# Row sums of a feed-forward input taken two places earlier, and one corner product of a Strassen pair split in halves around the second sum's product

## The chip, the core and the metric

The kernel runs on one core of one Trainium2 chip. The core has a matrix engine (TensorE, PE in the profile), a vector engine (DVE), a scalar engine (ACT), GpSimd (POOL) and a queue engine (SP), each with its own queue of instructions, and 16 DMA engines. The metric is the device time of one execution in microseconds. Three runs of the kernel before took 1920.91 to 1923.19 us, with a median of 1921.95 us. A change of about 0.2% is what such runs can tell from none.

## The reference, cut to what matters

Two layers, each a feed-forward network, a token mixing, and a second feed-forward network. The change touches the feed-forward input alone:

```
def swiglu(x, w_in, w_out):
    gate, up = jnp.split(x @ w_in, 2, axis=-1)
    return (jax.nn.silu(gate) * up) @ w_out
...
hn = rms_norm(h, g_ffn1[l]) * (1.0 + sc1) + sh1
h = h + 0.5 * (1.0 + gt1) * swiglu(hn, w_ffn1_in[l], w_ffn1_out[l])
```

There are 512 tokens, a model width of 1024 and a hidden width of 2816, that is 22 tiles of 128 hidden rows. All is float32.

## The kernel before

**Products.** A float32 operand is split into a high part (a rounded cast, on ACT, `nc.scalar.copy`) and a low part (the rest, a subtraction on DVE); `split`, lines 100 to 102, does both. A product then takes three passes through the matrix engine: high by high, high weights by low input, low weights by high input. Each weight tile of 128x1024 needs one cast on ACT and, after it, one subtraction on DVE before its third pass can run; the split pairs `wH` and `wL` live in a ring of four.

**A feed-forward input** (`ffn`, line 364). The hidden tiles come in pairs `p`, two tiles `j` to a pair. The first `n_first` pairs are multiplied directly: for each `j` a gate tile `pg` and an up tile `pu` come from the generator `projector` (line 278), then a block (lines 513 to 517) makes silu(gate) times up and splits it into `actH` and `actL`. `n_first` is 4 in the first feed-forward network, whose weights begin to arrive at the start of the program, and 2 in the other three. Their first three direct tiles are multiplied during the step before, so five follow in the network itself, each of 48 passes of 256 columns.

**The Strassen pairs.** All later pairs go through `pair_in` (line 449), which computes gate and up tiles of a pair with seven half-size products in place of eight. `prod` (line 436) is one such product: 2 hidden tiles by 4 row tiles by 3 passes, 24 passes of 256 columns. On the input side the products need sums and differences of rows of the input, `P1`, `P2`, `T3` and `T4`, made once for each network on DVE: `whole(0)` and `whole(1)` (line 406) join high and low parts of the rows again, four instructions each; `combine` (line 414) makes one of the four with two instructions and then splits it (one cast on ACT, one subtraction on DVE). On the weight side a pair loads four quarter tiles `A(i, k)`, two of them with an accumulating DMA on POOL (`plus`), and forms sums on DVE (lines 464 and 474).

One pair in order, before the change: `S`=A10+A11 by P1 into `pF` (line 457); copy `up` from `pF`; A00 (`a11`) by rows B11 into `pD` (461); copy `s1` from `pD` on ACT (463); `S` plus a11 on DVE (464); `flush()`, which runs the last product of the pair before (T4, line 486); `S` by P2 on top of `pD` (466); copy `s2` from `pD` (468); A01 (`a12`) by B21 into `pG` (470), the corner product; `gate` from `pG` and `s1` (472); `S` plus a12 (474); `S3` by T3 on top of `pD` (477); `S` by B22 into `pF` (479). `S` by P2 may not write `pD` before `s1` has been copied out of it. In the first Strassen pair nothing waits to be flushed.

**When the sums are made.** `when` (line 502) gives each of the six pieces a place `m` among the direct tiles: `beside(2 * j)` comes between `pg` and `pu` of tile `j`, `beside(2 * j + 1)` after its block. With `n_first` = 2 the places are 1 and 3 for the two `whole`, then 4, 5, 6 and 7 for P1, P2, T3 and T4.

**What orders the work.** A scheduler lays out each engine's queue ahead of time: of what it takes to be ready it prefers what stands earlier in the program. On the chip each queue runs in that order. `tc.issue_after(x)` puts what is written inside it behind the instruction `x` in that engine's queue, without a wait for its end. One shared tile `crep` (the conditioning vector, line 166) has the slot that also holds the sums P1 and T3 where `n_first` is 2; its load and its silu on ACT follow in the program after the first group of pairs.

## Time and profile before

| | us |
|---|---|
| median of three runs | 1921.95 |
| the profiled execution, its own time | 1922.28 |
| its span in the profile | 1920.5 |
| PE busy | 1884.7 |
| DVE busy | 1400.5 |
| ACT busy | 838.1 |

Times in the views are counted from the span's start. The three feed-forward inputs with two direct pairs end their direct tiles at about 673 us (second network of the first layer), 1021 us (first of the second layer) and 1617 us (second of the second layer); they are called the first, second and third place below. In the lists a row gives the start, the duration, the engine, the source line, the operation, the tiles written and read, the shape and the count, and in brackets the idle time before it with what ended it. Busy PE time is modelled: the passes follow each other more closely than their durations say, so the distance between starts tells more than the busy share.

### The profile page before, as it was taken

Reading aid. Unit: us, or ns where it says so; the run is one execution under the profiler, and the core shown is the slowest. Engines: PE = TensorE matmul, PEld = TensorE weight load, DVE = VectorE, ACT = ScalarE, POOL = GpSimd, SP = SyncE. Lnnn points to the kernel's source line nnn. Section 1 sums busy time; section 2 is a strip of 40 time slices with the busy share of each in tenths; the row PEclk is TensorE's granted clock in tenths of the full one; section 3 lists DMA queues with packets and bytes.
Section 4 is the critical chain, followed back from the end, with each engine's and each line's share of the span. In section 5 each row is a group of like instructions: output and inputs, shape, how many; then the busy total and the mean of one; then the engine's idle time right before and its main releaser. Section 6 shows DMA issues by size and latency. Waiting matters only on the chain. (4 is left out here: it accounts for less than half of the span.)

```text
span 1920.5 us, 37038 instructions
## 1 busy us (share of the span) xinstructions
PE 1884.7 (98%) x15504; PEld 1747.4 (91%) x15504; DVE 1400.5 (73%) x2181; ACT 838.1 (44%) x1264; POOL 130.9 (7%) x212
## 2 busy tenths in 40 slices
PE   8999999999999999999999999999999999999999
PEld 7998899997889999899899989989878899988998
DVE  7687687758976777777867777876598677773862
ACT  4443355356322554155345514544552234532551
POOL 0101100000000001100100020010000000110000
PEclk9999999999999999999999999999999999999999
DMA  7767877421322476877726688781212306765741
GB/s 299 250 165 227 264 194 237 156 69 46 79 60 62 122 198 178 296 201 197 258 73 182 169 264 236 199 278 41 88 54 50 98 23 184 183 212 136 197 139 59
DMA packets 104326, 308.46 MB, mean 161 GB/s; under 512 B 23392, under 2 KB 24416, under 8 KB 103136
## 3 DMA queue, kind: packets, MB, share of 16 engines
q1 hardware_dynamic: 75936, 203.33, 32.2%
q0 software_dynamic: 28224, 102.77, 21.4%
q8 instruction: 121, 1.98, 0.4%
q14 instruction: 45, 0.37, 0.1%
HBM read 302.66 MB, written 3.41 MB: 159 GB/s over the span
## 5 line engine op out<-in xcount | busy, mean ns | idle before, releaser
L101 ACT CAST wH<-wraw 128x1024 fp32r<-128x1024 f32 (+2 forms) x292 | 268.3, 922 | 511.7 <-PE ps_mm L91 175.2
L102 DVE TENSOR_TENSOR wL<-wraw,wH 128x1024 fp32r<-128x1024 f32 (+2 forms) x292 | 308.2, 1059 | 106.7 <-ACT wH L101 105.1
L90 PE MATMUL ps_mm<-actH,wH 128*128 128x512 f32 (+1 forms) x784 | 288.5, 368 | 0.0
L91 PE MATMUL ps_mm<-actL,wH 128*128 128x512 f32 (+1 forms) x784 | 288.0, 367 | 0.0
L92 PE MATMUL ps_mm<-actH,wL 128*128 128x512 f32 (+1 forms) x784 | 288.0, 367 | 0.0
L441 PE MATMUL ps_d<-comH,wH 128*128 128x256 f32 x816 | 228.9, 280 | 4.4 <-ACT s L463 3.6
L443 PE MATMUL ps_d<-comH,wL 128*128 128x256 f32 x816 | 227.3, 279 | 0.0
L442 PE MATMUL ps_d<-comL,wH 128*128 128x256 f32 x816 | 227.3, 279 | 0.0
L98 PE MATMUL ps_mm<-hnH,wH 128*128 128x256 f32 x1040 | 213.6, 286 | 5.8 <-ACT hnH L101 2.9
L98 PE MATMUL ps_mm<-hnL,wH 128*128 128x256 f32 x1040 | 211.8, 283 | 0.0
L98 PE MATMUL ps_mm<-hnH,wL 128*128 128x256 f32 x1040 | 209.3, 281 | 0.5 <-DVE wL L102 0.5
L163 DVE SCALAR_TENSOR_TENSOR wada<-wada,crep 128x1024 f32<-128x1024 f32 x140 | 167.9, 1220 | 46.3 <-DMA wada<-in_wadaT 46.0
L102 DVE TENSOR_TENSOR wL<-sum,wH 128x1024 fp32r<-128x1024 f32 x102 | 124.9, 1225 | 75.8 <-ACT wH L101 75.6
L98 PEld LDWEIGHTS ps_mm<-hnH,wH 128*128 128x128 f32 x1040 | 159.3, 189 | 16.7 <-issue 8.2
L101 ACT CAST wH<-sum 128x1024 fp32r<-128x1024 f32 x102 | 107.5, 1054 | 152.0 <-PE ps_d L442 71.4
L92 PEld LDWEIGHTS ps_mm<-actH,wL 128*128 128x128 f32 x784 | 147.8, 188 | 24.4
L90 PEld LDWEIGHTS ps_mm<-actH,wH 128*128 128x128 f32 x784 | 147.8, 189 | 24.2
L91 PEld LDWEIGHTS ps_mm<-actL,wH 128*128 128x128 f32 x784 | 147.8, 189 | 24.2
L98 PEld LDWEIGHTS ps_mm<-hnL,wH 128*128 128x128 f32 x1040 | 160.0, 189 | 6.7 <-issue 5.7
L98 PEld LDWEIGHTS ps_mm<-hnH,wL 128*128 128x128 f32 x1040 | 159.8, 190 | 4.0 <-issue 2.9
L441 PEld LDWEIGHTS ps_d<-comH,wH 128*128 128x128 f32 x816 | 155.2, 190 | 6.9 <-ACT s L463 5.1
L442 PEld LDWEIGHTS ps_d<-comL,wH 128*128 128x128 f32 x816 | 155.3, 190 | 0.0
(402 smaller groups left out, 4245.5 us busy)
## 6 DMA issues: line engine op xcount, KB each, us to landing
wada<-in_wadaT POOLq DMA_DIRECT2D x128, 512.0 KB, 4.9
wraw<-in_wmi SPq DMA_DIRECT2D x40, 512.0 KB
wraw<-in_w2p SPq DMA_DIRECT2D x36, 512.0 KB
wraw<-in_w1p SPq DMA_DIRECT2D x32, 512.0 KB
wraw<-in_w1o SPq DMA_DIRECT2D x32, 384.0 KB
wraw<-in_w2o SPq DMA_DIRECT2D x32, 384.0 KB
wraw<-in_w1i SPq DMA_DIRECT2D x20, 512.0 KB
wraw<-in_w1o SPq DMA_DIRECT2D x32, 320.0 KB
```

Of the source, the lines that this page charges most:

```text
L90: mm(acc, wH, xH, start=start, stop=False)
L91: mm(acc, wH, xL, start=False, stop=False)
L92: mm(acc, wL, xH, start=False, stop=stop)
L98: mm(acc[:, sl], w[a][:, k], x[b][:, sl], start=start and n == 0 and sl is HALVES[0], stop=stop and n == 2, skip_group_check=True)
L101: nc.scalar.copy(hi, src)
L102: nc.vector.tensor_sub(lo, src, hi.bitcast(F32))
L163: stt(w, w, 1.0, crep, ALU.mult, ALU.mult, accum_out=out_)
L441: mm(pt[:, i], wH, x[k][0], start=start and i + k == 0, stop=False, skip_group_check=True)
L442: mm(pt[:, i], wH, x[k][1], start=False, stop=False, skip_group_check=True)
L443: mm(pt[:, i], wL, x[k][0], start=False, stop=k == 3, skip_group_check=True)
```

## The change

Where `n_first` is 2, the six pieces of the sums go to places 0 to 5 in place of 1, 3, 4, 5, 6, 7. In the first Strassen pair of these three networks, the load and the split of a12 go ahead of the split of `S` for P2; the corner product into `pG` is done in two halves, the first hidden tile ahead of `S` by P2 and the second behind it; the cast of `S` for P2 is queued behind the copy `s1` on ACT; and on PE the product of P2 goes behind the first half, the second half behind it, and `S` by B22 behind that. The first network, with four direct pairs, is left as it was.

```
-            def prod(pt, w, x, start):
-
-                for i in range(2):
+            def prod(pt, w, x, start, parts=(0, 1)):
+
+                for i in parts:
...
-                        mm(pt[:, i], wL, x[k][0], start=False, stop=k == 3, skip_group_check=True)
+                        last = mm(pt[:, i], wL, x[k][0], start=False, stop=k == 3, skip_group_check=True)
+                return last
...
-                nc.scalar.copy(s1, pD)
+                copied = nc.scalar.copy(s1, pD)
                 tt(S, S, a11, ALU.add)
+
+                alone = p == n_first == 2
+                if alone:
+                    a12 = raw(A(0, 1))
+                    right = hl(a12)
+                    front = prod(pG, right, B21, True, (0,))
                 flush()
-                prod(pD, hl(S), P2, False)
+                with tc.issue_after(copied.ins) if alone else nullcontext():
+                    second = hl(S)
+                with tc.issue_after(front.ins) if alone else nullcontext():
+                    middle = prod(pD, second, P2, False)
                 s2 = half_("s2")
                 nc.scalar.copy(s2, pD)
-                a12 = raw(A(0, 1))
-                prod(pG, hl(a12), B21, True)
+                if alone:
+                    with tc.issue_after(middle.ins):
+                        back = prod(pG, right, B21, False, (1,))
+                else:
+                    a12 = raw(A(0, 1))
+                    back = prod(pG, hl(a12), B21, True)
...
-                prod(pF, hl(S), B22, False)
+                with tc.issue_after(back.ins) if alone else nullcontext():
+                    prod(pF, hl(S), B22, False)
...
-            when = {8 * (n_first == 4) + m: n for m, n in ((1, 0), (3, 1), (4, "P1"), (5, "P2"), (6, "T3"), (7, "T4"))}
+            turns_ = (9, 11, 12, 13, 14, 15) if n_first == 4 else (0, 1, 2, 3, 4, 5)
+            when = dict(zip(turns_, (0, 1, "P1", "P2", "T3", "T4")))
```

## The prediction

> **What bounds the kernel.** I read the page first, then who PE waits for, then the list of instructions around the longest waits.

> ```profile
> span 1920.5 us, 37038 instructions
> PE 1884.7 (98%) x15504; PEld 1747.4 (91%) x15504; DVE 1400.5 (73%) x2181; ACT 838.1 (44%) x1264; POOL 130.9 (7%) x212
> ```
> ```profile
> PE ps_g L443 <- DVE wL L102: 4.5, 3, 2.6
> PE ps_d L441 <- ACT s L463: 3.6, 2, 1.8
> ```

> PE bounds the kernel: 98% busy, so a change counts only where PE stops or runs at less than its pace. The two longest entries of PE's list of waits are exactly what the change touches: the corner product waiting for the low half of a12 (three times, once in each place), and P2's product waiting for the copy `s1` (two times). Together 8.1 us of idle time. That is not the whole price. What each place costs is seen from the first pass of the first pair (into `ps_f`) to that of the next pair, beside PE's undisturbed pace in the direct tiles:

> ```profile
> L98 PE MATMUL ps_mm<-hnH,wH x78: 274/276/284, 646.6 to 672.7; 128*128 128x256 f32 x78
> ```
> ```profile
> L441 PE MATMUL ps_f<-comH,wH x8: 276/276/276, 673.3 to 675.7; 128*128 128x256 f32 x8
> ```
> ```profile
> L441 PE MATMUL ps_f<-comH,wH x8: 281/281/281, 695.1 to 697.6; 128*128 128x256 f32 x8
> ```
> ```profile
> L441 PE MATMUL ps_f<-comH,wH x8: 276/276/276, 1021.0 to 1023.4; 128*128 128x256 f32 x8
> ```
> ```profile
> L441 PE MATMUL ps_f<-comH,wH x8: 276/276/276, 1042.2 to 1044.6; 128*128 128x256 f32 x8
> ```
> ```profile
> L441 PE MATMUL ps_f<-comH,wH x8: 276/276/281, 1616.8 to 1619.4; 128*128 128x256 f32 x8
> ```
> ```profile
> L441 PE MATMUL ps_f<-comH,wH x8: 276/276/276, 1639.8 to 1642.2; 128*128 128x256 f32 x8
> ```

> The first row counts one pass in three: 77 steps of three in 26.1 us, 0.113 us a pass. The first pair has six products of 24 passes (its seventh is flushed into the next pair): 144 passes, 16.3 us. The places take 21.8, 21.2 and 23.0 us (695.1 less 673.3, 1042.2 less 1021.0, 1639.8 less 1616.8). So 5.5, 4.9 and 6.7 us are lost, 17.1 us in all, twice the listed idle time.

> **The other half is the clock.** The granted clock in stretches of 3.41 us, laid on the edges of those at half clock:

> ```profile
> 681.26:684.67 3.41, 1.62 (x14) 1.41 (x13) 3.00 (x3) 1.53 (x2) 0.00 (x0) 1.00 0.95 205
> 684.67:688.09 3.42, 3.42 (x18) 3.42 (x18) 0.00 (x0) 0.08 (x1) 0.00 (x0) 0.50 0.98 363
> 1026.01:1029.42 3.41, 0.85 (x8) 0.65 (x6) 3.41 (x5) 2.85 (x4) 0.87 (x1) 1.00 0.65 166
> 1029.42:1032.83 3.41, 3.37 (x16) 3.37 (x16) 2.26 (x2) 0.63 (x2) 0.00 (x0) 0.50 1.02 270
> 1623.34:1626.75 3.41, 1.56 (x11) 1.36 (x11) 3.41 (x4) 2.09 (x3) 0.86 (x1) 1.00 0.50 80
> 1626.75:1630.17 3.42, 2.77 (x13) 2.77 (x14) 1.34 (x2) 0.60 (x2) 0.00 (x0) 0.50 1.01 267
> 1630.17:1633.58 3.41, 3.41 (x18) 3.41 (x18) 0.00 (x0) 0.82 (x1) 0.28 (x1) 0.50 0.78 312
> 585.69:589.10 3.41, 2.30 (x21) 2.04 (x20) 2.55 (x4) 1.78 (x4) 0.00 (x0) 1.00 0.28 86
> 589.10:592.52 3.42, 2.99 (x28) 2.75 (x26) 1.44 (x3) 0.40 (x1) 0.00 (x0) 1.00 0.54 140
> ```

> The first column after the length is PE's busy time, the third from the end the clock. Four stretches, one, one and two by place, run at 0.50. Each costs half its length, 1.71 us: 6.8 us together. The stretches before those at 0.50 had PE busy for 1.62, 0.85 and 1.56 us; the one from 585.69, with 2.30 us, was followed by one at 1.00. So 1.62 us of work in a stretch and less halves the clock for the next, 2.30 does not, and the bound lies between. (The stretch from 1626.75 is at 0.50 itself and holds a wait; after it the clock stayed down.) [...]

> **The wait for a12, and the wait for `s1`.** PE in the first place, and the same waits in the other two:

> ```profile
> 678.65 0.28 PE L443 MATMUL ps_d<-hnH,wL 128*128 128x256 f32 x1
> ```
> ```profile
> 678.99 0.28 PE L442 MATMUL ps_g<-hnL,wH 128*128 128x256 f32 x1
> 680.21 0.38 PE L443 MATMUL ps_g<-hnH,wL 128*128 128x256 f32 x1 [0.94 <-DVE wL L102]
> ```
> ```profile
> 681.49 0.28 PE L441 MATMUL ps_g<-hnH,wH 128*128 128x256 f32 x1
> 683.57 0.38 PE L441 MATMUL ps_d<-comH,wH 128*128 128x256 f32 x1 [1.79 <-ACT s L463]
> ```
> ```profile
> 1029.46 0.58 PE L443 MATMUL ps_g<-hnH,wL 128*128 128x256 f32 x1 [2.60 <-DVE wL L102]
> ```
> ```profile
> 1624.05 0.38 PE L443 MATMUL ps_g<-hnH,wL 128*128 128x256 f32 x1 [0.94 <-DVE wL L102]
> ```
> ```profile
> 1627.40 0.58 PE L441 MATMUL ps_d<-comH,wH 128*128 128x256 f32 x1 [1.79 <-ACT s L463]
> ```

> PE's queue already has the corner product split: 13 of its passes come ahead of P2's product, although the program writes it behind. So splitting the product on PE is hardly new (12 in place of 13); what is new is the order on ACT and DVE. From start to start the first wait is 1.22 us less a pass of 0.11, 1.11; the second 2.08 less 0.11, 1.97: 0.17 more than the idle column, which counts from a modelled end. The five waits then are 8.06 us by the idle column and 8.9 us with 0.17 added to each. With the clock's 6.8 that is 15.7 of the 17.1 us; 1.4 us are spread over small things, and I leave them lost.

> **Why these waits stand, and what moves.**

> ```profile
> 675.76 1.06 ACT L168 ACTIVATE crep<-crep 128x1024 f32<-128x1024 f32 x1 [3.24 <-DMA crep<-in_crep]
> 676.73 1.03 ACT L101 CAST wH<-sum 128x1024 fp32r<-128x1024 f32 x1
> ```
> ```profile
> 681.98 1.04 ACT L101 CAST wH<-sum 128x1024 fp32r<-128x1024 f32 x1 [1.32 <-DVE sum L474]
> 682.93 0.58 ACT L463 COPY s<-ps_d 128x512 f32<-128x512 f32 x1
> ```
> ```profile
> 673.14 1.22 DVE L102 TENSOR_TENSOR comL<-q,comH 128x1024 fp32r<-128x1024 f32 x1
> ```
> ```profile
> 677.80 1.23 DVE L102 TENSOR_TENSOR wL<-sum,wH 128x1024 fp32r<-128x1024 f32 x1 [0.57 <-ACT wH L101]
> 678.94 1.22 DVE L102 TENSOR_TENSOR wL<-wraw,wH 128x1024 fp32r<-128x1024 f32 x1
> ```

> The last sum (T4) leaves DVE at 674.36, behind schedule, and the weights of the pair queue behind it; a12 is last, done at 680.16, 0.05 us before PE goes on. On ACT the copy `s1`, possible from 678.93 (678.65 plus 0.28), stands behind two casts, an activation that waited 3.24 us for `crep`, and the cast of `S` plus a12, which itself waits for DVE.

> *Sums earlier.* Nothing is added: 16 instructions and four splits move. DVE has room for them:

> ```profile
> 647.10 1.23 DVE L102 TENSOR_TENSOR wL<-wraw,wH 128x1024 fp32r<-128x1024 f32 x1 [2.94 <-ACT wH L101]
> 649.01 0.69 DVE L515 SCALAR_TENSOR_TENSOR silu<-silu,ps_mm 128x512 f32<-128x512 f32 x1 [0.69 <-ACT silu L514]
> ```
> ```profile
> 652.18 2.49 DVE L411 TENSOR_TENSOR x<-hnH,hnL 128x512 f32<-128x512 f32 x4
> ```

> DVE was idle from 644.16 to 647.10 with all rows of the input made; the eight joining sums, 0.60 us each (2.49 for four that overlap a little), began only at 652.18. Begun at 644.2 they and the two of P1 end at 650.2 (ten by 0.60), 650.8 with the silu product between them; the subtraction of the next direct weight tile, which comes later in the program now, then ends at 652.0. PE needs it at 646.6 plus 50 passes of 0.113, 652.25. Just in time, so zero, with a risk of some tenths. The sums thus begin 8 us ahead of before and, I estimate, end at least 4 ahead, with T4 off DVE before 671: a12 is split in time and its three waits (4.48 us idle) go. What is late next is in the next paragraph. The load of a12 stands earlier in the program but passes no other issue on SP, and POOL's accumulating loads are not passed; the load of `crep` shares a slot with T3 and so can only come earlier.

> *P2's split behind `s1`.* This is the one wait that the change adds. On ACT nothing late stands ahead of the copy any more, so it starts when B11's product ends. Counted from the start of its last pass: copy from 0.28 to 0.86; the cast of `S` (1.03) begins 0.10 before the copy ends, as 682.93 does after 681.98 plus 1.04, and ends at 1.79; the subtraction starts 0.04 later (677.80 after 676.73 plus 1.03) and takes 1.23: 3.06; PE goes on 0.05 later, 3.11. Twelve passes of the first half fill PE to 12 by 0.113 plus 0.11, 1.47; P2's third pass, the first to need the low half, would be due at 1.70. Lost: 1.41 us a place, 4.2 us in all, as two waits of about 0.36 and 1.05. Behind the waiting pass PE holds the rest of P2 and, by order, the second half and B22, none of which may overtake. Below, this wait can hardly go under 0.4 (copy and cast alone); above, a DVE instruction in the way adds 1.2 us. I take 1.41: the rows give it directly. In the worst stretch of 3.41 us PE then works 2.0 us by starts, 2.3 as the busy column counts it (0.17 more at each of two waits): as much as the 2.30 that kept the clock. I expect the full clock.

> *Second half and T3.* The second half lasts 1.36 us (12 by 0.113) and covers the copy `s2` (0.58, the shape of `s1`) and its 0.28: nothing. Without that cover T3 would wait about 0.8. The cast of `S` plus a12 falls between P2's split and `s2`, so it no longer blocks a copy.

> **Sum.** 8.9 of waits and 6.8 of clock go, 4.2 come: 11.5 us. Against the profiled execution's own 1922.28 us, 1910.8; that execution lies 0.33 above the median, so 1910.4 us in the terms of the median.

> **Rivals.**
> - *The clock still falls.* A DVE instruction ahead of P2's subtraction, or an unlucky lie of the stretches, adds 1.2 us of wait and 1.7 us of clock in a place: 1913.3, 1916.2 or 1919.1 us with one, two or three places. For it: the worst stretch is near the bound. Against: DVE's queue is emptied early. Chance 0.22.
> - *The clock is not tied to waits this short.* [...] Were the stretches at half clock owed to something else, they would stay, and only 8.9 less 4.2 is gained: 1917.2 us. Against it, every halved stretch here follows a stretch with a wait of these. Chance 0.04.
> - *The moved sums starve the direct tiles.* If the sums cannot begin at 644.2 but all ten and P1's split (10 by 0.60 plus 1.22, 7.2 us) come ahead of a subtraction that before ended at 648.33, against a need at 652.25, PE waits 3.3 us, the clock falls too (1.7), and three places lose 15: the time is 1910.4 plus 15, 1925.4 us, slower. It decides from 3.9 us of sums after 647.1. Against: 2.94 idle us ahead of it. Chance 0.06.
> - *P2's wait is small* (0.4 a place, because its low half is ready sooner than its order says): 3.0 us better, 1907.4. Chance 0.06.
> - *The change does little*: the queues come out much as before, since PE already has the split, or a new wait of equal size stands elsewhere. Within 2 us of 1921. Chance 0.06.

> The forecast has the other 0.56, with 1909 to 1912.5 as its own range. Going from 1906.5 to 1917.0 takes in the small wait, one or two falls of the clock and most of the forecast, and leaves out under 2 in 10. About 0.2% (3.8 us) is what can be told from no change: below 1918.1 lie the forecast, the small wait, most of the falling clock and the rule's case, 0.86; between, 0.08; above, 0.06.

> **What would show it.** In the changed kernel's list of waits, `ps_g` on `wL` is gone; `ps_d` waits for `wL` three times at 0.9 to 1.1 us and for `wH` at 0.2 to 0.4; no stretch at 0.50 in the three places; first pair to next pair 17.5 to 18.5 us; T4's subtraction ends by 671. Wrong would be a direct tile waiting for `wL`, a stretch at 0.50, or `s1` again behind a cast.

## The result, and the profile after

The changed kernel took 1912.2 us (median of 4 runs, 1910.95 to 1915.12) against 1921.81 us for the kernel before (4 runs, 1920.91 to 1923.19): a ratio of 0.9943, with a 95% interval of 0.9926 to 0.9961 (the two medians alone give 0.9950). The profiled execution took 1913.21 us, with a span of 1911.2 us in place of 1920.5.

First the totals of the profile after, then the entries of PE's list of waits that concern the pairs (engine, tile and line waited at, what was waited for; then total us, times, longest):

```profile
span 1911.2 us, 37042 instructions
PE 1878.8 (98%) x15504; PEld 1741.7 (91%) x15504; DVE 1399.8 (73%) x2181; ACT 837.0 (44%) x1264; POOL 130.7 (7%) x212
```
```profile
PE ps_d L443 <- DVE wL L102: 2.3, 3, 0.8
...
PE ps_g L443 <- DVE wL L102: 1.1, 1, 1.1
...
PE ps_d L441 <- ACT wH L101: 0.8, 3, 0.3
```

PE's busy time fell by 5.9 us (from 1884.7). The three waits of `ps_g` for a12 in the places are gone; the one `ps_g` entry left lies elsewhere, at 1169 us. P2's product (`ps_d`) now waits three times for the high half and three times for the low half of `S`. No wait for `s1` is left in the places. The three places, by the first pass of the first pair and of the next pair (PE's rows in order of time):

```profile
674.11 0.28 PE L441 MATMUL ps_f<-comH,wH 128*128 128x256 f32 x1
...
692.28 0.28 PE L441 MATMUL ps_f<-comH,wH 128*128 128x256 f32 x1
...
1018.75 0.28 PE L441 MATMUL ps_f<-comH,wH 128*128 128x256 f32 x1
...
1036.73 0.28 PE L441 MATMUL ps_f<-comH,wH 128*128 128x256 f32 x1
...
1612.23 0.28 PE L441 MATMUL ps_f<-comH,wH 128*128 128x256 f32 x1
...
1630.40 0.28 PE L441 MATMUL ps_f<-comH,wH 128*128 128x256 f32 x1
```

The places take 18.17, 17.98 and 18.17 us, where they took 21.84, 21.18 and 23.03: 3.67, 3.20 and 4.86 us less, 11.7 us together. In each of them the wait looks the same; PE and ACT in the first place:

```profile
679.48 0.28 PE L443 MATMUL ps_d<-hnH,wL 128*128 128x256 f32 x1
...
680.84 0.28 PE L443 MATMUL ps_g<-hnH,wL 128*128 128x256 f32 x1
681.37 0.39 PE L441 MATMUL ps_d<-comH,wH 128*128 128x256 f32 x1 [0.26 <-ACT wH L101]
681.60 0.28 PE L442 MATMUL ps_d<-comL,wH 128*128 128x256 f32 x1
682.63 0.39 PE L443 MATMUL ps_d<-comH,wL 128*128 128x256 f32 x1 [0.75 <-DVE wL L102]
```
```profile
679.79 0.59 ACT L464 COPY s<-ps_d 128x512 f32<-128x512 f32 x1 [2.17 <-PE ps_d L443]
680.27 1.05 ACT L101 CAST wH<-sum 128x1024 fp32r<-128x1024 f32 x1
```

ACT now stands idle for 2.17 us until B11's product ends, copies `s1` at once, and only then casts `S`: in the kernel before, the copy came at 682.93. The clock, in the stretch that holds the wait and the one after it (the second column is PE's busy time, the third from the end the granted clock):

```profile
680.74:684.15 3.41, 2.40 (x19) 1.99 (x18) 2.80 (x3) 1.52 (x2) 0.00 (x0) 1.00 0.00 0
684.15:687.57 3.42, 3.42 (x32) 3.42 (x31) 2.25 (x3) 2.63 (x4) 0.00 (x0) 1.00 0.78 210
```

With 2.40 us of work in the worst stretch the clock stays at 1.00, and there is no stretch at 0.50 in any of the three places.

The span became shorter by 9.3 us, not by 11.7. The same starts, compared with those of the kernel before (673.3, 695.1, 1021.0, 1042.2, 1616.8, 1639.8), say where the other 2.4 us went: 0.8 before the first place, 0.6 between first and second, 0.9 between second and third, 0.1 after. The first part is a sum of small differences, among them a longer stretch at half clock near the start of the program (6.83 us from 21.54, after 3.41 from 22.49 in the kernel before); the 0.9 is a single pair:

```profile
1162.35 1.05 ACT L101 CAST wH<-first 128x1024 fp32r<-128x1024 f32 x1 [9.00 <-DMA first<-in_w1p]
```
```profile
1169.10 0.38 PE L443 MATMUL ps_g<-hnH,wL 128*128 128x256 f32 x1 [1.12 <-DVE wL L102]
```

In that pair, which the change does not alter, ACT's queue stood 9.00 us for a load, and PE paid 1.12 us for it later. Whether this belongs to the change is asked below.

### The profile page after: what moved, and what is told of

Read it like the earlier page. It is cut to its first block, busy times and chain, and to the rows that moved or that the text cites. A ratio compares the mean times of both kernels' runs of the same rounds, so it can differ in the third digit from the quotient of the medians.

```text
span 1911.2 us, 37042 instructions
## 1 busy us (share of the span) xinstructions
PE 1878.8 (98%) x15504; PEld 1741.7 (91%) x15504; DVE 1399.8 (73%) x2181; ACT 837.0 (44%) x1264; POOL 130.7 (7%) x212
## 3 DMA queue, kind: packets, MB, share of 16 engines
HBM read 302.66 MB, written 3.41 MB: 160 GB/s over the span
## 5 line engine op out<-in xcount | busy, mean ns | idle before, releaser
L101 ACT CAST wH<-wraw 128x1024 fp32r<-128x1024 f32 (+2 forms) x292 | 268.4, 922 | 512.6 <-PE ps_mm L91 176.8
L102 DVE TENSOR_TENSOR wL<-wraw,wH 128x1024 fp32r<-128x1024 f32 (+2 forms) x292 | 308.1, 1058 | 96.9 <-ACT wH L101 95.8
L441 PE MATMUL ps_d<-comH,wH 128*128 128x256 f32 x816 | 226.8, 278 | 1.6 <-ACT wH L101 0.8
L443 PE MATMUL ps_d<-comH,wL 128*128 128x256 f32 x816 | 225.8, 277 | 2.3 <-DVE wL L102 2.3
L442 PE MATMUL ps_d<-comL,wH 128*128 128x256 f32 x816 | 225.5, 276 | 0.0
L98 PE MATMUL ps_mm<-hnH,wH 128*128 128x256 f32 x1040 | 214.0, 286 | 5.1 <-ACT hnH L101 2.9
L98 PE MATMUL ps_mm<-hnL,wH 128*128 128x256 f32 x1040 | 211.8, 283 | 0.0
L98 PE MATMUL ps_mm<-hnH,wL 128*128 128x256 f32 x1040 | 209.5, 281 | 0.5 <-DVE wL L102 0.5
L102 DVE TENSOR_TENSOR wL<-sum,wH 128x1024 fp32r<-128x1024 f32 x102 | 124.8, 1224 | 74.9 <-ACT wH L101 74.7
L98 PEld LDWEIGHTS ps_mm<-hnH,wH 128*128 128x128 f32 x1040 | 159.5, 190 | 16.1 <-issue 8.2
L101 ACT CAST wH<-sum 128x1024 fp32r<-128x1024 f32 x102 | 107.5, 1054 | 140.3 <-PE ps_d L442 60.1
L98 PEld LDWEIGHTS ps_mm<-hnL,wH 128*128 128x128 f32 x1040 | 160.2, 190 | 6.7 <-issue 5.7
L98 PEld LDWEIGHTS ps_mm<-hnH,wL 128*128 128x128 f32 x1040 | 160.1, 190 | 4.1 <-issue 2.9
L441 PEld LDWEIGHTS ps_d<-comH,wH 128*128 128x128 f32 x816 | 153.2, 188 | 3.9 <-ACT wH L101 1.4
L443 PEld LDWEIGHTS ps_d<-comH,wL 128*128 128x128 f32 x816 | 153.2, 188 | 2.9 <-DVE wL L102 2.9
```

Of the source, the lines that this page charges most:

```text
L98: mm(acc[:, sl], w[a][:, k], x[b][:, sl], start=start and n == 0 and sl is HALVES[0], stop=stop and n == 2, skip_group_check=True)
L101: nc.scalar.copy(hi, src)
L102: nc.vector.tensor_sub(lo, src, hi.bitcast(F32))
L441: mm(pt[:, i], wH, x[k][0], start=start and i + k == 0, stop=False, skip_group_check=True)
L442: mm(pt[:, i], wH, x[k][1], start=False, stop=False, skip_group_check=True)
L443: last = mm(pt[:, i], wL, x[k][0], start=False, stop=k == 3, skip_group_check=True)
```

## The experiments

The theory after the result (A): each place costs its 16.3 us plus the waits that the queues of ACT and DVE fix, and a stretch at half clock where a stretch is left with too little work (1.62 us and less in the profile before); the change removes a12's waits by the earlier sums, `s1`'s by the order of the pair. Rivals: one of the two parts does all of it and the other nothing or harm; and the clock has nothing to do with waits of one or two microseconds. Ratios are to the kernel before, timed beside them on the same chip; its median was 1922.33 us beside the first four and 1921.99 us beside the next three.

**The sums alone.** The pair is written as before; only the places of the sums change.

```
-            when = {8 * (n_first == 4) + m: n for m, n in ((1, 0), (3, 1), (4, "P1"), (5, "P2"), (6, "T3"), (7, "T4"))}
+            turns_ = (9, 11, 12, 13, 14, 15) if n_first == 4 else (0, 1, 2, 3, 4, 5)
+            when = dict(zip(turns_, (0, 1, "P1", "P2", "T3", "T4")))
```

> Only the places of the sums change; the first pair is as before. My theory (the two parts are substitutes: either empties the queue ahead of a12 and the copy): no wait for a12's low half, the copy s1 still behind the cast of S plus a12 but for one cast alone, so P2 starts about 0.4 us late in each place and nothing waits for the low half of S: 17.0 to 17.4 us from first pair to next, 1908 to 1911 us. Rival (the gain comes from the order in the pair): the waits for a12 and for s1 stay and with them the halved clock, 1917 to 1922 us.

Measured: 1909.07 us, ratio 0.9935 (0.9923 to 0.9946). The places take 17.10, 17.10 and 17.37 us, without a stretch at half clock: 2.75 us less in all than in the changed kernel. Its rows of PE and of ACT in the first place:

```profile
681.29 0.28 PE L441 MATMUL ps_g<-hnH,wH 128*128 128x256 f32 x1
681.66 0.38 PE L441 MATMUL ps_d<-comH,wH 128*128 128x256 f32 x1
681.89 0.28 PE L442 MATMUL ps_d<-comL,wH 128*128 128x256 f32 x1
682.00 0.29 PE L443 MATMUL ps_d<-comH,wL 128*128 128x256 f32 x1
```
```profile
673.34 1.06 ACT L101 CAST wH<-sum 128x1024 fp32r<-128x1024 f32 x1 [2.47 <-DVE sum L464]
...
680.08 1.05 ACT L101 CAST wH<-sum 128x1024 fp32r<-128x1024 f32 x1 [0.47 <-PE ps_d L442]
681.03 0.58 ACT L463 COPY s<-ps_d 128x512 f32<-128x512 f32 x1
```

The cast of `S` for P2 is done at 674.40, before the pair has begun, and P2's third pass follows the second after 0.11 us: its weights wait for nobody. The one thing left in the way is the cast of `S` plus a12 at 680.08, behind which the copy of `s1` stands until 681.03; PE loses 0.26 us (681.66 less 681.29 less a pass). In the third place the product of T3 also waits 0.36 us for the copy `s2`. So the earlier sums clear the a12 wait and nearly all of the `s1` wait by themselves.

**The order of the pair alone.** The new `pair_in` with the old places of the sums.

```
-            turns_ = (9, 11, 12, 13, 14, 15) if n_first == 4 else (0, 1, 2, 3, 4, 5)
-            when = dict(zip(turns_, (0, 1, "P1", "P2", "T3", "T4")))
+            when = {8 * (n_first == 4) + m: n for m, n in ((1, 0), (3, 1), (4, "P1"), (5, "P2"), (6, "T3"), (7, "T4"))}
```

> Only the pair's order changes; the sums stand where they were. My theory (substitutes): a12 is split ahead of S on both engines and is ready in time, the copy s1 is prompt, and what remains is the wait of P2 for its own split, 1.35 us a place as in the changed kernel: 17.9 to 18.5 us from first pair to next, 1911 to 1915 us. Rival (the sums carry the gain): DVE is still behind, a12 or S comes late and the clock falls, 1917 to 1922 us.

Measured: 1915.69 us, ratio 0.9963 (0.995 to 0.9976). Places 18.83, 18.29 and 19.18 us, no half clock in them: two of the three places and the time are a little above what was expected, and still under the rival's 1917. The first place:

```profile
682.21 0.38 PE L441 MATMUL ps_d<-comH,wH 128*128 128x256 f32 x1 [0.81 <-ACT wH L101]
683.47 0.38 PE L443 MATMUL ps_d<-comH,wL 128*128 128x256 f32 x1 [0.76 <-DVE wL L102]
```
```profile
679.62 0.62 ACT L531 CAST actH<-silu 128x512 fp32r<-128x512 f32 x1 [1.75 <-DVE silu L530]
...
680.63 0.59 ACT L464 COPY s<-ps_d 128x512 f32<-128x512 f32 x1
```

Without the earlier sums DVE is late, ACT's cast `actH` waits for it, and the copies queue behind that cast: 0.55 us more wait for `wH` in two of the three places. The order too is worth something alone, 6.6 us by the medians, against 13.3 for the sums alone and 9.6 for both. The parts do not add: they cure the same waits, and the order puts a wait of its own in their place.

**The cast of `S` not held back.** The changed kernel with one line less.

```
-                with tc.issue_after(copied.ins) if alone else nullcontext():
-                    second = hl(S)
+                second = hl(S)
```

> The changed kernel, but the cast of S for P2 is not held behind the copy s1. My theory (this holding is the whole remaining loss): P2 no longer waits for the low half of S; since the cast of S plus a12 can then stand ahead of the copy, P2 still starts about 0.4 us late: 16.9 to 17.4 us from first pair to next, 3 us less in all, 1908 to 1910.5 us. Rival (without the holding the copy is late again as before): waits of 1 to 2 us for s1 with a halved clock, 1914 to 1920 us.

Measured: 1911.77 us, ratio 0.9945 (0.9933 to 0.9957); places 17.49, 17.21 and 17.21 us, 2.4 us less than in the changed kernel. P2's wait for its own halves is gone in them. What is left is a wait of 0.20 us for `s1`:

```profile
679.40 1.06 ACT L101 CAST wH<-sum 128x1024 fp32r<-128x1024 f32 x1 [1.26 <-PE ps_d L442]
680.37 0.58 ACT L464 COPY s<-ps_d 128x512 f32<-128x512 f32 x1
```

Freed, the scheduler moved the other cast, that of `S` plus a12, ahead of the copy. The median is only 0.4 us lower, and the ratio not lower at all, where 3 us less were expected. In its profile the pair near 1160 us, which stands behind late loads in the changed kernel too, took 2.95 us longer than in the kernel before; that is one profile, and the times do not tell the two kernels apart.

**The corner product whole, ahead of P2.**

```
-                    front = prod(pG, right, B21, True, (0,))
+                    front = back = prod(pG, right, B21, True)
...
-                if alone:
-                    with tc.issue_after(middle.ins):
-                        back = prod(pG, right, B21, False, (1,))
-                else:
+                if not alone:
```

> The changed kernel, but the corner product runs whole ahead of P2's. My theory: its 24 passes (2.7 us) cover the split of S, so P2 loses under 0.2 us; then T3 has no cover for the copy s2 and waits 0.5 to 0.8 us: 17.0 to 17.5 us from first pair to next, 1909 to 1911 us. Rival (the second half behind P2 is worth its place): T3's wait is over 1.4 us and the time is that of the changed kernel or more, 1912 us and up.

Measured: 1913.34 us, ratio 0.9954 (0.9942 to 0.9966); places 17.75, 17.74 and 17.77 us. Twenty-four passes do cover the copy, the cast and the subtraction of P2, whose wait is gone, and the copy `s2` has lost its cover. The listed wait does not stand at T3, where it was expected, but at the product of `S` by B22, of which PE takes two passes ahead of T3:

```profile
687.67 0.28 PE L443 MATMUL ps_d<-comH,wL 128*128 128x256 f32 x1
688.56 0.39 PE L441 MATMUL ps_f<-hnH,wH 128*128 128x256 f32 x1 [0.62 <-ACT wH L101]
...
689.05 0.39 PE L441 MATMUL ps_d<-comH,wH 128*128 128x256 f32 x1
```
```profile
687.46 1.05 ACT L101 CAST wH<-sum 128x1024 fp32r<-128x1024 f32 x1 [2.67 <-DVE sum L485]
688.41 0.58 ACT L478 COPY s<-ps_d 128x512 f32<-128x512 f32 x1
```

The cast at 687.46 is that of `S` plus a12 for B22. It waited 2.67 us for DVE's sum, and the copy `s2` stands behind it: copied at 688.99, it lets T3 begin at 689.05. From P2's last pass (687.67) to that start are 1.38 us, with three passes due, 0.34: 1.04 us lost, of which 0.62 is listed. So the halves save about 1.0 us a place by starts, and cost 1.45 by starts through the wait in front of P2 (1.0 as listed). In the total this does not show: the median lies 1.1 us above the changed kernel's, where the rival put it (1912 and up), though not for the rival's reason, a wait of T3 over 1.4 us. The intervals do not tell the two apart.

**Both casts placed.** The cast of `S` is free, and that of `S` plus a12 is held behind `s1`.

```
-                with tc.issue_after(copied.ins) if alone else nullcontext():
-                    second = hl(S)
+                second = hl(S)
...
+                with tc.issue_after(copied.ins) if alone else nullcontext():
+                    last_ = hl(S)
                 with tc.issue_after(back.ins) if alone else nullcontext():
-                    prod(pF, hl(S), B22, False)
+                    prod(pF, last_, B22, False)
```

> The changed kernel with the cast of S for P2 free to go early and the cast of S plus a12 held behind the copy s1 in its stead. My theory (the copy must not stand behind that cast, and P2's split need not stand behind the copy): no wait of P2 at all: 16.8 to 17.1 us from first pair to next, 0.3 us a place better than with the cast merely free, 1908 to 1910.5 us. Rival (some other order on the queues holds P2): 17.4 us a place or more, 1911 us and up.

Measured: 1909.32 us, ratio 0.9936 (0.9924 to 0.9949); places 16.73, 16.72 and 16.73 us, which is 0.4 over the 16.3 of 144 passes at full pace. DVE and ACT in the first place:

```profile
675.09 1.23 DVE L102 TENSOR_TENSOR wL<-sum,wH 128x1024 fp32r<-128x1024 f32 x1
```
```profile
679.71 0.59 ACT L464 COPY s<-ps_d 128x512 f32<-128x512 f32 x1 [1.33 <-PE ps_d L443]
```

The low half of `S` is ready at 676.32, and the copy starts as soon as B11's product ends. This and the sums alone lie some 3 us under the changed kernel by their medians; all three intervals overlap, so the times alone separate none of the three. The places do separate these two from the changed kernel, by 0.8 to 1.4 us in each, in one profile of each of the two.

**The copy of `s1` made twice, and four times.** Two kernels that lengthen P2's wait and nothing else; the copies write the same values again. The edit is that for two copies; for four, the 1 is a 3.

```
                 copied = nc.scalar.copy(s1, pD)
+                alone = p == n_first == 2
+                for _ in range(1 if alone else 0):
+                    copied = nc.scalar.copy(s1, pD)
```

> The changed kernel with the copy s1 written once more in the same three pairs (same values), so that P2's wait grows by the 0.48 us between two copies, to about 1.85 us. Theory A (the clock falls once a stretch of 3.41 us holds less than about 2 us of work): PE works about 1.9 us by the busy column in the worst stretch, near the bound; the clock may fall in none or one of the places: 18.5 us a place, 20.2 where it falls. Theory B (the clock does not follow such waits): 18.5 us in all three, 1.4 us over the changed kernel.

> The changed kernel with the copy s1 written three more times in the same three pairs (same values), so that P2's wait grows by 1.44 us, to about 2.8 us. Theory A: the worst stretch has about 0.9 us of work where it holds the whole wait, and the clock halves in at least two of the three places: 21.0 to 21.5 us there, 6 to 10 us over the changed kernel in all. Theory B: no fall, 19.5 us in all three, 4.3 us over the changed kernel.

Measured: 1918.8 us, ratio 0.9975 (0.9959 to 0.999), with two copies, and 1924.08 us, ratio 1.001 (1.0 to 1.0021), with four. With two, PE waits 0.88 and 0.76 us in every place, 0.63 more than in the changed kernel: the second copy starts 0.62 us after the first (680.43 and 681.05, in the first place), not the 0.48 expected. Yet the places take 20.15, 18.56 and 20.20 us: two falls of the clock, where none or one was expected. The stretches of the clock, two for each place:

```profile
680.56:683.97 3.41, 1.77 (x14) 1.37 (x12) 1.35 (x2) 2.94 (x4) 0.00 (x0) 1.00 0.01 1
683.97:687.38 3.41, 3.41 (x16) 3.41 (x17) 2.30 (x3) 1.04 (x1) 0.00 (x0) 0.50 0.39 95
1028.72:1032.13 3.41, 2.33 (x18) 2.13 (x19) 3.11 (x3) 1.22 (x2) 0.00 (x0) 1.00 0.00 0
1032.13:1035.54 3.41, 3.41 (x33) 3.41 (x32) 2.29 (x4) 2.99 (x4) 0.06 (x1) 1.00 0.89 251
1622.64:1626.05 3.41, 1.77 (x13) 1.37 (x12) 2.20 (x2) 2.12 (x3) 0.00 (x0) 1.00 0.00 0
1626.05:1629.46 3.41, 3.41 (x18) 3.41 (x17) 2.30 (x3) 1.05 (x1) 0.00 (x0) 0.50 0.66 175
```

The same pair of waits leaves 1.77 us of work in a stretch where it falls wholly inside one, and the next runs at 0.50; in the second place the edge at 1028.72 cuts it, 2.33 us are left, and the clock stays. The falls cost 1.4 us each beyond the wait (20.15 less 18.17 less 0.63, and 20.20 less 18.17 less 0.63, 1.35 and 1.40). With four copies the waits are 2.12 and 0.76, all three places have a stretch at 0.50, and they take 21.66, 21.40 and 21.41 us, 10.2 us over the changed kernel in all: the whole gain is gone. So lengthening this wait is enough to take the clock down; the rival (theory B) is out. Two stretches of these kernels lie closest to the bound, one of the second place with four copies and one of the mixing step with two:

```profile
1029.67:1033.08 3.41, 1.79 (x13) 1.59 (x14) 2.57 (x3) 1.75 (x2) 0.00 (x0) 1.00 0.00 0
```
```profile
1527.06:1530.48 3.42, 1.82 (x16) 1.63 (x14) 1.32 (x2) 1.05 (x1) 0.00 (x0) 1.00 0.56 149
```

The first was followed by a stretch at 0.50, the second by one at 1.00.

**Both kernels once more**, one execution each, to see what stands from run to run (no edit).

> The kernel before, unchanged, profiled once more. Theory A (the waits are fixed by the queues, the clock by where free-running stretches lie): the five waits stand at the same 0.94, 1.79, 2.60, 0.94 and 1.79 us of idle time within 0.1, while the number of stretches at half clock in the three places may be 3 to 5 in place of 4, so the places sum to 64 to 68 us. For the pair that starts near 1167 us: 17.4 us again if the loss of 0.5 to 3 us seen there in every changed kernel is owed to the changes, 17.8 or more if it is scatter of a load. Theory B (the losses scatter as a whole): the waits themselves move by over 0.3 us.

> The changed kernel, unchanged, profiled once more. Theory A: the waits of P2 at 0.26 and 0.75 us of idle time in each place again, no stretch at half clock there, 17.9 to 18.2 us a place; what differs from the first profile lies in the program's start, in the pair near 1162 us and in the mixing step. Theory B: the waits or the places move by over 0.3 us.

Measured: 1918.21 us for the kernel before, 1913.46 us for the changed one; one more execution of the kernel before, timed beside these, took 1928.81 us, and no trace shows why. The changed kernel repeated its places, 18.29, 18.17 and 17.98 us, with 0.26 and 0.75 to 0.76 us of wait in each. The kernel before did not: 21.39, 17.59 and 21.56 us. In its second place a12's wait was 0.56 us in place of 2.60, and no stretch ran at 0.50. In its third place the waits were the same, 0.94 and 1.81 us, but one stretch ran at 0.50 in place of two, and it took 1.47 us less. The ACT queue of the second place, in the first profile and in the second:

```profile
1008.79 1.05 ACT L101 CAST wH<-sum 128x1024 fp32r<-128x1024 f32 x1 [4.94 <-DMA sum<-in_w1p]
...
1024.59 1.05 ACT L101 CAST wH<-wraw 128x1024 fp32r<-128x1024 f32 x1
```
```profile
1006.87 1.05 ACT L101 CAST wH<-sum 128x1024 fp32r<-128x1024 f32 x1 [2.65 <-DMA sum<-in_w1p]
...
1022.67 1.05 ACT L101 CAST wH<-wraw 128x1024 fp32r<-128x1024 f32 x1
```

The accumulating load of `S`, issued at 1001.16 and at 1001.10, took 7.5 us to land in the first profile and 5.7 in the second. The cast of `S` moved with it, and everything behind it on ACT, a12's cast 16 us later too, came about 1.9 us earlier. That part of theory A (the queues fix the waits) fails for the second place of the kernel before: a load fixes it, and so it scatters. The sum of the places, 60.54 us, lies below the 64 to 68 expected. By these two profiles the gain in the places was 6.1 us (60.54 less 54.44), by the first two 11.7.

The pair near 1162 us is not settled by these runs. Beside the first profile of the kernel before it took 0.87 us more in the changed kernel, 0.45 with the sums alone, 1.48 with the order alone, 2.95 with the cast free, 0.85 with the corner whole, 2.78 and 0.75 with two and four copies, and 0.2 less with both casts placed and in each of these two repeats. The changed kernel had it both ways, so it does change from run to run; but the loss stands in seven of nine profiles with some part of the change and in neither of the two without, and whether the change makes it likelier stays open.

## Why the prediction was right, point by point

The forecast was 1910.4 us, from 11.5 us gained in the places; they gave 11.7, and the time was 1912.2. That 11.5 and 11.7 stand so close is in part luck: with the repeated profile of the kernel before, whose places lost less, the gain is 6.1. The medians, 9.6 us apart, lie between.

- *What the places cost, and why.* Right in its parts, with two limits. The waits of the first and third place are the queues' (they came again within 0.02 us), but that of the second, 2.60 us, was lengthened by a late load. The half clock is owed to the waits, as one and three copies more showed; each fall cost 1.35 to 1.62 us beyond its wait in those two kernels, not the 1.71 of the sum. The bound was put between 1.62 and 2.30 us of work; the runs narrow it, for the places and the mixing step, to between 1.79 and 1.82.
- *Sums earlier.* Right in its outcome, wrong in how. The first joining sum starts at 638.7, not 644.2 (13.5 us ahead of before, not 8), between the steps that make the rows; only `whole(0)` and half of P1 and P2 come ahead of the next weight tile's subtraction, and the four joins of `whole(1)` start at 653.0. So nothing was "just in time": the subtraction forecast to end at 652.0 starts at 647.92. T4 leaves DVE at 669.28, 5.1 us earlier (at least 4 and before 671 were forecast), and the low half of a12 at 673.82, 6 us before PE needs it.

```profile
L411 DVE TENSOR_TENSOR x<-hnH,hnL x8: 679/684/689, 638.7 to 654.8; 128x512 f32<-128x512 f32 x8
```
```profile
647.92 1.23 DVE L102 TENSOR_TENSOR wL<-wraw,wH 128x1024 fp32r<-128x1024 f32 x1 [0.68 <-ACT wH L101]
...
653.00 2.49 DVE L411 TENSOR_TENSOR x<-hnH,hnL 128x512 f32<-128x512 f32 x4
...
668.06 1.22 DVE L102 TENSOR_TENSOR comL<-q,comH 128x1024 fp32r<-128x1024 f32 x1
...
671.47 1.22 DVE L465 TENSOR_TENSOR sum<-sum,first 128x1024 f32<-128x1024 f32 x1
672.60 1.22 DVE L102 TENSOR_TENSOR wL<-wraw,wH 128x1024 fp32r<-128x1024 f32 x1
```

- *P2's split behind `s1`.* Forecast 1.41 us a place. From the last pass of B11 (679.48) to P2's third pass (682.63) are 3.15 us (forecast 3.11), with 1.70 due: 1.45. As listed idle time it is 0.26 and 0.75; the 0.9 to 1.1 that I named for the second was too high, since the list counts from the modelled end of P2's second pass, which itself starts late. The mechanism and the size hold. What I took as given is that this wait has to be there. `S` is finished at 672.69 (671.47 plus 1.22), and its cast could have gone then, as in the kernel with the sums alone; the change holds it for 7.6 us, until 680.27, behind a copy that it no longer threatened.
- *Second half and T3.* Nothing lost, as said. Without the cover 1.04 us are lost by starts, not 0.8: T3 does wait for `s2`, with two passes of B22 taken in ahead of it. And the cast of `S` plus a12, which was said to block a copy no longer, is then what `s2` stands behind.
- *The clock.* No stretch at half clock in the places, as forecast; 2.40 us of work in the worst stretch of the first place against the 2.3 worked out.
- *The sum.* The term that was off is the rest of the program, taken as unchanged: 2.4 us more there in the profiled execution, spread over it as shown above. It scatters: over the eleven profiles the span less the three places runs from 1853.8 us (both casts placed) to 1859.6 (corner whole), with 1854.5 and 1855.7 in the two of the kernel before and 1856.9 and 1857.0 in the two of the changed one. Whether the change adds to it can't be told from these. And the 21.18 us of the second place before, taken as the kernel's, were in part that run's: the same place took 17.59 once more.
- *Rivals.* The clock falling again: not in this kernel, but 0.63 us of wait a place away from it. The clock not tied to waits this short (1917.2 us, counted among the chances as the rule's case): no run shows such a rule; with two copies, waits of 0.88 and 0.76 us were followed by half clock in two of the three places. Direct tiles starved of their subtraction: none; the one wait of `ps_mm` for `wL`, 0.52 us at 991.54, stands in the kernel before too, at 993.97. P2's wait small: not here, but it is what the kernel with both casts placed does, at 16.7 us a place.

## What to carry to other kernels

Two edits that cure the same wait do not add up: run each alone, since the second may keep only its own cost (here the order holds back a cast that the earlier sums had already put out of the way, some 1 us a place). Before an instruction is tied behind another, ask when its inputs will be ready after the other edits of the same change. And a wait of one to two microseconds on the bounding engine is to be priced with the clock it may take down (1.35 to 1.62 us a fall here, beyond the wait), which depended here on where the wait fell (1.77 us of work left in a stretch, or 2.33, by the same two waits).
